# Output projection by block products: third's blocks in two tasks, the norm's weights on POOL, an earlier input load

## The chip, the core and the metric

The kernel runs on one NeuronCore of a Trainium2 chip. The metric is the time of one execution on the device in microseconds (us). The core's engines are TensorE (PE in the profile, its weight loads PEld), VectorE (DVE), ScalarE (ACT), GpSimd (POOL) and SyncE (SP), which here only issues DMAs. Each engine works through its own instructions in program order and waits on semaphores for the others.

## What is computed

One layer of a decoder trunk for one sequence of 512 tokens and a width of 2048 (all f32): a modulated RMSNorm, one wide input projection, latent attention and a spatial gating unit side by side, their gated sum `merged`, an output projection with a gated residual, and a final RMSNorm. The change lies in the last two lines:

```python
merged = jax.nn.sigmoid(g_mla) * y_mla + jax.nn.sigmoid(g_sgu) * y_sgu
x = x + gate[:, None] * (merged @ w_out[l])      # (512, 2048) @ (2048, 2048)
return rmsnorm(x, final_norm_g)                  # y * rsqrt(mean(y*y) + eps) * g
```

## The kernel before

Every f32 matrix product is done as three products of fp32r parts. A tile is split into a high part (a cast on ACT) and a low part (tile minus high part, on DVE); `hilo` (L139) is these two instructions, and `tt` (L122) is DVE's tensor_tensor. The engines' program order is the order in which the Python code issues the instructions; nothing reorders them.

**The output projection.** The 2048 output columns are four column groups of 512 (`columns(cg)`, L1564), the 512 tokens four blocks of 128 (n = 0 to 3), and the 16 chunks of `merged` are `mh[j]`, `ml[j]` (high and low, 128 x 512 tokens each). `left` and `right` are the two halves of 256 tokens. Column groups 0 and 3 are done plainly: `out_granule` (L1470) multiplies two chunks with a weight tile of 128 x 1024 into four PSUM banks, eight granules for each group. Column groups 1 and 2 are done together as a 2 x 2 block product (two halves of the tokens, of the 16 chunks and of the columns) with seven block products in place of eight. They run in the order `seven = (6, 1, 7, 2, 5, 3, 4)` (L1585), each in four granules of one weight tile of 128 x 1024; `steps` (L1587) lists the 28 pairs (product, granule). The sums and differences that this needs are made of three kinds of data:

- Of the chunks: `make_dsum(c)` (L1568) makes three combinations of the chunks c and c + 8 for products 6, 2 and 7 (s1, s2, s4). `make_third(c)` (L1578) makes left half minus right half of chunk c, splits it, and writes it over the right half of `mh[c]`, `ml[c]`. It is a sum on DVE, a difference on DVE, a cast on ACT and the low part on DVE, one behind the other.
- Of the weights: DMAs that add to what is in SBUF, issued by POOL (`chain_load`, `third_add`). `third_load` (L1602) first loads four plain tiles by SP into the space of s4h and s4l, and so waits until product 7 has read them.
- Of the results: `after(p, n2)` (L1691) combines the PSUM banks of the products, on ACT and DVE, into `y_of(col, half, n2)` for the column groups 1 and 2, two halves of the tokens and two blocks in each. They lie in the space of s1h and s1l. `gated` multiplies with the gate row `grow`, and `add_x` (L1683) has POOL issue a DMA that adds the block of x from DRAM.

**The order of work** (L1766). In step s the code first issues the weight split of step s + 2 (`split_step`, a cast on ACT and a low part on DVE, 1024 wide; three buffers, so the cast waits until PE has finished step s - 1), then the weight load three tiles ahead (`take`, on SP), then the 12 matmuls of the granule (six for each of two token blocks; `granule`, L1652), and then the tasks that hang on this step in the dictionary `tasks`. Tasks of a step stand in the order in which they were put in. So the tasks of step s lie between the splits of steps s + 2 and s + 3 on ACT and DVE. Before, the thirds hang on (1,1), (1,3), (7,0), (7,2) and the four granules of product 2; the plain group 3 is finished by `plain_residual(3, n)` at (6,0), (6,2), (1,0) and (7,1), and group 0 between the granules of group 3 (L1634).

**The norm.** A residual is `ps * grow` and then `+ y` (x was loaded into y before). `norm_part` (L1552) squares y on ACT with a sum along the row into `ssy`, and then multiplies y with the norm's weights `gfb` on DVE. For the left token blocks in column groups 1 and 2 the second step is left to the end: `finish_row` (L1720) scales with the row's 1/rms, by ACT ("act"), by DVE's tensor_scalar, or with the weights in one DVE instruction ("last"), and has SP store each piece.

**The end** (L1781). `after(3, .)` forms the right blocks; product 4 then runs for block 2 as a whole and for block 3 in two halves of 256 columns. `left_rows(m)` finishes the two left blocks and `norm_of(2, 1, m)` norms column group 2 of the two right ones, both behind product 4's first four granules; then each right block gets its last residual, norm and stores.

## Time and profile before

| | us |
|---|---|
| median of 3 runs (lowest to highest) | 1613.58 (1613.2 to 1614.93) |
| the profiled execution | 1613.45 |
| its span, first to last instruction | 1611.8 |
| busy time of PE / DVE / ACT / POOL | 1587.3 / 1218.1 / 783.8 / 126.0 |
| first matmul of the block products | 1511.43 |
| end of the last matmul | 1595.68 |

Times in the profile are us from the start of the span. A row of the timeline gives start, duration, engine, line in the kernel, operation, out <- in by the program's names (without buffer numbers), shapes and types, and in brackets how long the engine had been idle and which instruction released it. The line is often that of a helper (L123 is `tt`, L140 the cast in `hilo`), so the names of the tiles tell what it is: w0, w1, w2 are the buffers of split weights, wraw and raw unsplit ones, sig is a temporary, s1 and s4 hold the combined chunks and later the results, gbc is `grow`. PE's durations overlap: matmuls of 512 columns start 0.23 us apart and last 0.39.

### The profile page before, as it was taken

The numbers are of one execution on the slowest core, as the hardware profiler recorded it, in microseconds if no ns is written. First come the engines' busy times: TensorE is split into PE (matmuls) and PEld (weight loads), VectorE is DVE, ScalarE is ACT, GpSimd is POOL, SyncE is SP. The second block draws the span as 40 slices with busy tenths as digits, with TensorE's granted clock in tenths as the row PEclk, the third lists the DMA queues.
The fourth block names the chain that finished last, engine by engine and source line by source line (L and its number), as shares of the span: only waits on it lengthen the run. The fifth ranks groups of instructions, "written<-read, shape, count | busy, mean of one in ns | idle before, by whom it ended". The sixth has DMA issues, their size and how long they took to land.

```text
span 1611.8 us, 27090 instructions
## 1 busy us (share of the span) xinstructions
PE 1587.3 (98%) x10688; PEld 1478.9 (92%) x10688; DVE 1218.1 (76%) x1815; ACT 783.8 (49%) x1311; POOL 126.0 (8%) x152
## 2 busy tenths in 40 slices
PE   9999999999999999999999999999999999999996
PEld 8888889999999999999999999999888898888865
DVE  8989679658777777777777777666878887867776
ACT  4443334455545454454555554554655545534444
POOL 0000000001111111111111101112000000000011
PEclk9999999999999999999999999999999999999998
DMA  9988488568899998898887988888422322338587
GB/s 379 353 298 314 171 281 322 169 201 208 218 249 252 233 247 214 233 255 213 228 248 199 271 244 221 231 196 198 133 92 82 105 89 83 97 137 255 132 216 175
DMA packets 127519, 340.14 MB, mean 211 GB/s; under 512 B 14600, under 2 KB 36384, under 8 KB 121120
## 3 DMA queue, kind: packets, MB, share of 16 engines
q1 hardware_dynamic: 106064, 269.72, 47.9%
q0 software_dynamic: 21328, 68.69, 24.3%
q8 instruction: 84, 1.38, 0.3%
q14 instruction: 43, 0.35, 0.1%
HBM read 314.43 MB, written 23.93 MB: 210 GB/s over the span
## 4 chain that ended last, share of the span: by engine, by line
PE 87%; DVE 4%; DMA 3%; issue 3%; ACT 3%; POOL 1%; SPq 0%; DVEq 0%; ACTq 0%; POOLq 0%
PE ps L1256 14%; PE ps L1258 14%; PE ps L1257 14%; PE ps L136 14%; PE ps L137 13%; PE ps L135 13%; PE ps L1418 1%; DMA lat<-v_d 1%; PE ps L1381 1%; PE ps L1382 1%; DMA wsr<-in_wsT 1%; DMA wraw<-in_w 1%; DVE w1l L123 1%; PE ps L819 0%; DMA s1l<-in_xn 0%
## 5 line engine op out<-in xcount | busy, mean ns | idle before, releaser
L1256 PE MATMUL ps<-hh,w0h 128*128 128x256 f32 x416 | 118.5, 285 | 0.9 <-DVE lat L123 0.9
L1257 PE MATMUL ps<-hl,w0h 128*128 128x256 f32 x416 | 117.7, 283 | 0.0
L1258 PE MATMUL ps<-hh,w0l 128*128 128x256 f32 x416 | 117.7, 283 | 0.0
L1256 PE MATMUL ps<-hh,w2h 128*128 128x256 f32 x400 | 113.5, 284 | 0.0
L1256 PE MATMUL ps<-hh,w1h 128*128 128x256 f32 x400 | 113.4, 283 | 0.0
L1258 PE MATMUL ps<-hh,w2l 128*128 128x256 f32 x400 | 113.2, 283 | 0.0
L1257 PE MATMUL ps<-hl,w1h 128*128 128x256 f32 x400 | 113.2, 283 | 0.0
L1257 PE MATMUL ps<-hl,w2h 128*128 128x256 f32 x400 | 113.2, 283 | 0.0
L1258 PE MATMUL ps<-hh,w1l 128*128 128x256 f32 x400 | 113.2, 283 | 0.0
L126 DVE SCALAR_TENSOR_TENSOR wada<-wada,cact 128x2048 f32<-128x2048 f32 x47 | 107.1, 2281 | 0.0
L123 DVE TENSOR_TENSOR w2l<-raw,w2h 128x1024 fp32r<-128x1024 f32 x60 | 73.4, 1224 | 41.2 <-ACT w2h L638 39.1
L105 ACT CAST w0h<-wraw 128x1024 fp32r<-128x1024 f32 (+3 forms) x69 | 63.6, 922 | 82.3 <-PE ps L137 44.2
L105 ACT CAST w1h<-wraw 128x1024 fp32r<-128x1024 f32 (+3 forms) x69 | 58.6, 849 | 91.8 <-PE ps L137 36.3
L106 DVE TENSOR_TENSOR w0l<-wraw,w0h 128x1024 fp32r<-128x1024 f32 (+3 forms) x69 | 72.7, 1054 | 36.9 <-ACT w0h L105 36.5
L106 DVE TENSOR_TENSOR w1l<-wraw,w1h 128x1024 fp32r<-128x1024 f32 (+3 forms) x69 | 67.0, 971 | 35.7 <-ACT w1h L105 34.7
L618 POOL DMA_DIRECT2D wraw<-in_wh x67 | 59.3, 939 | 439.4 <-DVE w0l L123 212.4
L135 PE MATMUL ps<-w0h,hh 128*128 128x256 f32 (+3 forms) x288 | 92.7, 322 | 0.0
L136 PE MATMUL ps<-w0l,hh 128*128 128x256 f32 (+3 forms) x288 | 92.7, 322 | 0.1
L137 PE MATMUL ps<-w0h,hl 128*128 128x256 f32 (+3 forms) x288 | 92.4, 321 | 0.0
L135 PE MATMUL ps<-hh,w1h 128*128 128x512 f32 x226 | 89.8, 397 | 0.0
L136 PE MATMUL ps<-hl,w1h 128*128 128x512 f32 x226 | 88.3, 391 | 0.8 <-DVE hl L126 0.8
L123 DVE TENSOR_TENSOR w1l<-wraw,w1h 128x1024 fp32r<-128x1024 f32 x48 | 58.8, 1225 | 40.0 <-ACT w1h L638 37.5
(479 smaller groups left out, 5525.1 us busy)
## 6 DMA issues: line engine op xcount, KB each, us to landing
raw<-in_wh SPq DMA_DIRECT2D x105, 512.0 KB, 6.9
wada<-in_wada SPq DMA_DIRECT2D x47, 1024.0 KB, 7.4
wraw<-in_wh POOLq DMA_DIRECT2D x67, 512.0 KB, 7.1
wraw<-in_wh SPq DMA_DIRECT2D x45, 512.0 KB, 8.0
raw<-in_wh POOLq DMA_DIRECT2D x42, 512.0 KB, 8.2
wraw<-in_wo SPq DMA_DIRECT2D x28, 512.0 KB, 4.1
half<-in_w SPq DMA_DIRECT2D x35, 256.0 KB, 5.4
wraw<-in_w SPq DMA_DIRECT2D x16, 512.0 KB, 8.5
```

The source lines that it names most:

```text
L105: self.nc.scalar.copy(hi[:, :n], raw[:, :n])
L106: self.nc.vector.tensor_tensor(out=lo[:, :n], in0=raw[:, :n], in1=hi[:, :n].bitcast(F32), op=ALU.subtract)
L123: DVE.tensor_tensor(out=out, in0=in0, in1=in1, op=op)
L126: DVE.scalar_tensor_tensor(out=out, in0=in0, scalar=scalar, in1=in1, op0=op0, op1=op1, **kw)
L135: PE.matmul(ps, ah, bh, start=start, stop=False)
L136: PE.matmul(ps, ah, bl, start=False, stop=False)
L137: PE.matmul(ps, al, bh, start=False, stop=stop)
L618: q_.dma_start(t, wh[h, n, q // 10 - 1], **eng)
L1256: PE.matmul(ps, wH[:, sl], xh, start=st, stop=False, skip_group_check=True)
L1257: PE.matmul(ps, wH[:, sl], xl, start=False, stop=False, skip_group_check=True)
L1258: PE.matmul(ps, wL[:, sl], xh, start=False, stop=sp, skip_group_check=True)
L1381: PE.matmul(ps, q2[:, q], krh[:, :n], start=False, stop=False)
```

## The change

Three edits, all in the output projection:

1. `make_third` becomes two tasks. `third_diff(c)` makes the difference into a tile of its own (`dif`, 128 x 256); `third_split(c)`, one step later, casts it and makes the low part. Chunk 0 begins at (1,2), chunk 1 at (7,0), and then one at each step up to (2,2).
2. `norm_part` becomes `square` (ACT) and `gain` (the product with `gfb`, on DVE or on the engine given). For the plain groups the gain is a task one step behind the square; group 0's gains move in the same way, and `plain_residual(3, n)` moves to (6,0), (6,2), (6,3) and (1,0), its gains to (6,1), (6,3), (1,0) and (1,1). For column groups 1 and 2 of the left blocks, and for column group 2 of the right ones, the gain is done by POOL (six tiles of 128 x 512). The left blocks' pieces that were "last" become tensor_scalar on DVE.
3. x for column group 1 of the right blocks is loaded by SP when product 1 begins, as a plain load, and added with the gate by `residual` after product 3, in place of `gated` and an adding DMA of POOL. In the end section both `left_rows` come behind product 4's second granule, and both `norm_of(2, 1, m)` behind its fourth.

```diff
--- before.py
+++ after.py
@@ -1549,17 +1549,17 @@
         load_before(go[3, 2 + i], chain_load, i, 11)
         load_before(go[3, min(4 + i, 7)], chain_load, i, 12)
 
-    def norm_part(n, part, cols, y, last):
+    def square(n, part, y):
         junk = nt(tp, [P, S], F32, "sig", bufs=3)[:, :y.shape[-1]]
         ACT.activation(junk, y, AF.Square, accum_out=ssy[:, n, part:part + 1])
-        if not last:
-            tt(y, y, gfb[:, cols], ALU.mult)
-
-    def residual(n, part, cols, y, ps, last=False):
+
+    def residual(cols, y, ps):
         t = nt(tp, [P, S], F32, "sig", bufs=3)[:, :y.shape[-1]]
         tt(t, ps, grow[:, cols], ALU.mult)
         tt(y, t, y, ALU.add)
-        norm_part(n, part, cols, y, last)
+
+    def gain(cols, y, eng=None):
+        (eng or DVE).tensor_tensor(out=y, in0=y, in1=gfb[:, cols], op=ALU.mult)
 
     def columns(cg, o=0, w=S):
         return slice(cg * S + o, cg * S + o + w)
@@ -1575,11 +1575,16 @@
         for n, src in (("s1", b[:, right]), ("s2", a[:, left]), ("s4", b[:, left])):
             hilo(dsum[n + "h"][:, c], dsum[n + "l"][:, c], src)
 
-    def make_third(c):
+    def third_diff(c):
         a = nt(tp, [P, S], F32, "sig", bufs=3)
         tt(a, mh[c].bitcast(F32), ml[c].bitcast(F32), ALU.add)
-        tt(a[:, left], a[:, left], a[:, right], ALU.subtract)
-        hilo(mh[c][:, right], ml[c][:, right], a[:, left])
+        dif[c] = nt(dp[0].p, [P, 256], F32, "dif")
+        tt(dif[c], a[:, left], a[:, right], ALU.subtract)
+
+    def third_split(c):
+        hilo(mh[c][:, right], ml[c][:, right], dif.pop(c))
+
+    dif = {}
 
 
     seven = (6, 1, 7, 2, 5, 3, 4)
@@ -1627,7 +1632,11 @@
         hilo(hi, lo, raw)
 
     def plain_residual(cg, n):
-        residual(n, cg and 1, columns(cg), yt[cg][:, n], plain[cg][n])
+        residual(columns(cg), yt[cg][:, n], plain[cg][n])
+        square(n, cg and 1, yt[cg][:, n])
+
+    def plain_gain(cg, n):
+        gain(columns(cg), yt[cg][:, n])
 
     plain = {0: pso, 3: [bank_at(4 + k) for k in range(NB)]}
     for cg in (0, 3):
@@ -1636,6 +1645,8 @@
             if cg == 0 and i > 3:
                 make_dsum(i - 4)
             elif cg and i % 2 == 0:
+                if i > 0:
+                    plain_gain(0, i // 2 - 1)
                 make_dsum(4 + i // 2)
             elif cg:
                 plain_residual(0, i // 2)
@@ -1673,6 +1684,8 @@
         elif p == 1:
 
             yp[0], yp[1] = (nt(dp[0].p, [P, 2, 2 * S], F32, t) for t in ("s1h", "s1l"))
+            for n2 in range(2):
+                DMA.dma_start(y_of(1, 1, n2), xn[2 + n2][:, columns(1)])
             pair_banks["y"] = [bank_at(k) for k in (2, 3)]
         elif p == 5:
             pair_banks["w"] = [bank_at(k) for k in (4, 5)]
@@ -1702,8 +1715,6 @@
             gated(y, y, 2)
             add_x(0, n2, 2)
         elif p == 3:
-            gated(y_of(1, 1, n2), b, 1)
-            add_x(1, n2, 1)
             y = y_of(2, 1, n2)
             tt(y, y, b, ALU.subtract)
             gated(y, y, 2)
@@ -1715,7 +1726,8 @@
             add_x(0, n2, 1)
 
     def norm_of(col, half, n2):
-        norm_part(2 * half + n2, 2 if half else col + 1, columns(col), y_of(col, half, n2), half == 0)
+        square(2 * half + n2, 2 if half else col + 1, y_of(col, half, n2))
+        gain(columns(col), y_of(col, half, n2), nc.gpsimd)
 
     def finish_row(n, r, pieces):
 
@@ -1734,7 +1746,7 @@
         ACT.activation(r, r, AF.Sqrt, bias=eps, scale=1.0 / D)
         DVE.reciprocal(out=r, in_=r)
         finish_row(n, r, [(columns(cg), yt[cg][:, n] if cg in yt else y_of(cg, 0, n), k)
-                          for cg, k in ((0, "act"), (1, "last"), (2, "last"), (3, "act"))])
+                          for cg, k in ((0, "act"), (3, "act"), (2, "dve"), (1, "dve"))])
 
 
     tasks = {}
@@ -1743,9 +1755,13 @@
         tasks.setdefault((p, i), []).append(lambda: f(*a))
 
     for c in range(8):
-        task((1, 1, 7, 7, 2, 2, 2, 2)[c], (1, 3, 0, 2, 0, 1, 2, 3)[c], make_third, c)
-    for n, (p, i) in enumerate(((6, 0), (6, 2), (1, 0), (7, 1))):
-        task(p, i, plain_residual, 3, n)
+        at_ = (6, 8, 9, 10, 11, 12, 13, 14)[c]
+        task(*steps[at_], third_diff, c)
+        task(*steps[at_ + 1], third_split, c)
+    for n in range(4):
+        task(*steps[(0, 2, 3, 4)[n]], plain_residual, 3, n)
+        task(*steps[(1, 3, 4, 5)[n]], plain_gain, 3, n)
+    task(*steps[0], plain_gain, 0, 3)
     for i in range(4):
         task(6, min(i + 2, 3), chain_load, i, 22)
         task(2, min(i + 2, 3), chain_load, i, 21)
@@ -1780,6 +1796,8 @@
 
     for n2 in range(2):
         after(3, n2)
+    for n2 in range(2):
+        residual(columns(1), y_of(1, 1, n2), pair_banks["y"][n2])
     half = S // 2
     for n2 in range(2):
         n = 2 + n2
@@ -1790,19 +1808,21 @@
             ps = bank_at((6, 7, 0)[n2 + part])[:, :w]
             for i in range(4):
                 granule(4, i, [ps], [n2], slice(o, o + w))
-                if n2 == 0 and i == 3:
+                if (n2, i) == (0, 1):
                     for m in range(2):
                         left_rows(m)
+                if (n2, i) == (0, 3):
+                    for m in range(2):
                         norm_of(2, 1, m)
             yo = y[:, o:o + w]
             last = o + w == S
             if last:
                 DVE.tensor_reduce(out=r, in_=ssy[:, n, 0:3 + part], axis=AX.X, op=ALU.add)
                 ts(r, r, 1.0 / D, EPS, ALU.mult, ALU.add)
-            t = nt(tp, [P, S], F32, "sig", bufs=3)[:, :w]
-            tt(t, ps, grow[:, columns(1, o, w)], ALU.mult)
-            tt(yo, t, yo, ALU.add)
-            norm_part(n, 3 + part, columns(1, o, w), yo, last)
+            residual(columns(1, o, w), yo, ps)
+            square(n, 3 + part, yo)
+            if not last:
+                gain(columns(1, o, w), yo)
         ACT.activation(r, ssy[:, n, 3 + part:4 + part], AF.Sqrt, bias=r, scale=1.0 / D)
         DVE.reciprocal(out=r, in_=r)
         pieces = [(columns(0), yt[0][:, n], "act"), (columns(3), yt[3][:, n], "dve"), (columns(2), y_of(2, 1, n2), "dve")]
```

## The prediction

> **What bounds the kernel now.** I read first the chain of waits that ended last, by engine: it consists of matmuls, so up to the last matmul every idle moment of TensorE is lost time. The edits begin where the output projection's plain groups end; from there I read a table of stretches, one for each block product in the order 6, 1, 7, 2, 5, 3 (then 4) and one for what follows the last matmul. Its columns: stretch, length, busy time of PE, PEld, DVE, ACT and POOL, granted clock, DMA share, GB/s.
>
> ```profile
> PE 87%; DVE 4%; DMA 3%; issue 3%; ACT 3%; POOL 1%; SPq 0%; DVEq 0%; ACTq 0%; POOLq 0%
> ...
> 1511.43:1522.67 11.24, 11.24 (x50) 9.04 (x49) 8.87 (x11) 5.43 (x8) 2.54 (x3) 1.00 0.92 160
> 1522.67:1533.55 10.88, 10.88 (x49) 9.01 (x48) 7.69 (x10) 5.67 (x9) 0.00 (x0) 1.00 0.65 202
> 1533.55:1546.83 13.28, 11.93 (x50) 8.69 (x48) 9.12 (x14) 5.65 (x10) 0.00 (x0) 1.00 0.51 160
> 1546.83:1560.73 13.90, 13.14 (x48) 10.27 (x49) 10.81 (x15) 5.01 (x7) 6.03 (x7) 0.88 1.00 258
> 1560.73:1573.34 12.61, 11.70 (x49) 8.78 (x48) 10.08 (x15) 8.19 (x11) 2.56 (x3) 1.00 1.06 229
> 1573.34:1584.22 10.88, 10.88 (x49) 9.01 (x48) 10.79 (x12) 6.22 (x11) 1.70 (x2) 1.00 0.60 106
> 1595.68:1611.80 16.12, 0.00 (x0) 0.00 (x0) 7.51 (x20) 4.32 (x13) 0.00 (x0) 0.64 0.57 207
> ```
>
> Undisturbed, product 6 takes 11.24 us (four granules of 2.81) and product 1 takes 10.88 (2.72). Products 7 and 2 use the same kind of operands as 6, products 5 and 3 as 1; so 7, 2 and 5 lose 2.04, 2.66 and 1.73, in all **6.4 us**. That is the most that splitting the third's task can win. The timeline of PE shows whom it waited for, and a stretch after it the clock:
>
> ```profile
> 1534.23 0.50 PE L1661 MATMUL ps<-w0l,s4h 128*128 128x512 f32 x1 [0.28 <-DVE w0l L123]
> 1546.83 0.50 PE L1660 MATMUL ps<-w2h,s2h 128*128 128x512 f32 x1 [0.73 <-ACT w2h L140]
> 1548.09 0.50 PE L1661 MATMUL ps<-w2l,s2h 128*128 128x512 f32 x1 [0.76 <-DVE w2l L123]
> ...
> 1549.00:1552.00 3.00, 3.00 (x9) 2.32 (x8) 2.01 (x4) 2.30 (x3) 1.03 (x2) 0.50 0.93 311
> ```
>
> PE is late because the weights' splits are late, and behind two holes of 0.73 and 0.76 us the clock stood at 0.50 for 3 us: 1.5 of the 6.4 us. The splits are late because of how DVE and ACT take turns (their timelines, DVE first):
>
> ```profile
> 1518.38 1.23 DVE L123 TENSOR_TENSOR w1l<-wraw,w1h 128x1024 fp32r<-128x1024 f32 x1 [0.16 <-ACT w1h L140]
> 1519.52 0.68 DVE L123 TENSOR_TENSOR sig<-ps,gbc 128x512 f32<-128x512 f32 x1
> 1520.24 0.69 DVE L123 TENSOR_TENSOR y<-sig,y 128x512 f32<-128x512 f32 x1
> 1521.72 0.69 DVE L123 TENSOR_TENSOR y<-y,gfb 128x512 f32<-128x512 f32 x1 [0.79 <-ACT sig L1554]
> 1522.65 1.22 DVE L123 TENSOR_TENSOR w0l<-wraw,w0h 128x1024 fp32r<-128x1024 f32 x1 [0.24 <-ACT w0h L140]
> 1524.00 1.23 DVE L123 TENSOR_TENSOR w2l<-wraw,w2h 128x1024 fp32r<-128x1024 f32 x1
> 1528.76 1.22 DVE L123 TENSOR_TENSOR w1l<-wraw,w1h 128x1024 fp32r<-128x1024 f32 x1 [0.73 <-ACT w1h L140]
> 1530.62 0.42 DVE L123 TENSOR_TENSOR sig<-sig 128x256 f32<-128x256 f32 x1
> 1531.52 0.43 DVE L123 TENSOR_TENSOR g<-sig,b 128x256 fp32r<-128x256 f32 x1 [0.47 <-ACT b L140]
> 1532.95 1.23 DVE L123 TENSOR_TENSOR w0l<-wraw,w0h 128x1024 fp32r<-128x1024 f32 x1 [1.01 <-ACT w0h L140]
> ...
> 1520.96 0.63 ACT L1554 ACTIVATE sig<-y 128x512 f32<-128x512 f32 x1 [2.62 <-DVE y L123]
> 1521.59 1.03 ACT L140 CAST w0h<-wraw 128x1024 fp32r<-128x1024 f32 x1
> 1527.21 0.57 ACT L1695 COPY s1l<-ps 128x512 f32<-128x512 f32 x1
> 1527.68 1.05 ACT L140 CAST w1h<-wraw 128x1024 fp32r<-128x1024 f32 x1
> ```
>
> With a third in the granule, DVE makes the difference, waits 0.47 for ACT's cast, subtracts, then waits 1.01 for the next split's cast: 4.19 us from 1528.76 to 1532.95 where PE needs 2.72.
>
> **The thirds.** With the difference a granule ahead, a granule costs DVE 1.14 (1518.38 to 1519.52) for the split, 0.34 for the third's low part (0.43 less the same overlap of 0.09) and 0.72 + 0.34 for the next difference: 2.5 us, less than 2.72, and neither cast waits for DVE. I take the three products' waits as gone. What covers this is DVE's spare time.
>
> **The plain residuals.** Residual, Square on ACT, then the next split's cast on ACT: the cast stands behind the Square, and the Square behind the residual. From 1518.38 to 1522.65 that is 4.27 us, and the weighting with gfb at 1521.72 lies in the hole, free. The change takes it out of the hole and puts it, 0.60 us each, a granule later in front of the next residual; and the residuals move to granules 0, 2, 3 and 4. So the low parts of the splits start: (6,1) at 1512.0 (three tasks earlier, 0.6 of weighting is added; 1511.40 before); (6,2) 1.14 later; (6,3) 1517.4 (+4.28, one weighting still fits the hole); (1,0) 1519.2 (+1.14 + 0.60); (1,1) 1523.4 (+4.27); (1,2) 1528.3 (+4.27 + 0.60); (1,3) 1533.7 (+0.47 more, the copy of 1527.21). Before, the last two were 1524.00 and 1528.76. Each is ready 1.22 later. PE wants them with its second matmul, at 1528.3 and, 1.4 us late by then, at 1532.5: it waits 1.3 and 2.5 us, with 0.1 for each restart **4.0 us**. The new holes (about 0.9, 1.3 and 0.9) are larger than those that cost the clock before, so I add 1.5: **5.5 us lost in place of 6.4**.
>
> The Trainium skill, TensorE: Matmul & The Clock Gate, section HAM oscillation, gives as the rule that only idle gaps above some 3.4 us lower the clock; the 0.50 behind gaps of 0.73 and 0.76 us disagrees, and by the rule the 1.5 us would go (second rival).
>
> **The loads behind it.** Product 3's weights come by DMA, and there the gain is capped (a stretch; the two queues between 1545 and 1580 us with packets, MB and share of the 16 engines' time; then SP's, POOL's and ACT's rows):
>
> ```profile
> 1547.00:1577.50 30.50, 28.82 (x115) 22.33 (x116) 24.88 (x32) 15.53 (x20) 8.59 (x10) 0.94 1.04 239
> ...
> q0 software_dynamic: 1440, 4.72, 69.1%
> q1 hardware_dynamic: 835, 3.03, 24.9%
> ...
> 1545.89 0.81 SPq L1606 DMA_DIRECT2D s4h<-in_wo  x2
> 1548.33 0.85 POOL L1539 DMA_DIRECT2D raw<-in_wo  x1 [28.98 <-DVE w2l L123]
> 1577.99 1.05 ACT L140 CAST w0h<-s4l 128x1024 fp32r<-128x1024 f32 x1 [1.82 <-DMA s4l<-in_wo]
> ```
>
> The DMA engines are full for 30 us. The last weights of product 3 land at 1577.95, and cast, subtraction and matmuls follow closely; a faster PE would wait here. The loads at 1545.89 reuse s4h, so they start when product 7 ends: 4.0 + 1.5 - 1.1 (what 7 lost before its last matmul) = 4.4 us later. One accumulating load (the one of 1548.33, which waits only for the split of (2,0)) now runs before them. The accumulating queue, q0, took 69.1% of 35 us, 24 us, for 4.72 MB: 2.7 us for a block of 512 KB. So the last landing comes 4.4 - 2.7 = 1.7 us later. Today DVE is 1.0 us late for that block behind older splits, which it no longer is, and PE needs it only 0.5 us after it is ready; with these 1.5 us off, product 3 ends **0.2 us later**, though TensorE alone would be 0.9 earlier. The bounds: 0.9 earlier, if the loads keep up; 1.7 later, if none of that slack comes back.
>
> **The tail.** Before, the last x add decides (POOL's issues, the chain's DMA step, the Squares that follow):
>
> ```profile
> 1582.89 0.84 POOL L1686 DMA_DIRECT2D s1h<-in_xn  x1 [2.74 <-DVE s1h L123]
> 1587.97 7.06 DMA s1l<-in_xn
> 1595.11 0.63 ACT L1554 ACTIVATE sig<-s1l 128x512 f32<-128x512 f32 x1 [0.20 <-DMA s1l<-in_xn]
> 1598.22 0.63 ACT L1554 ACTIVATE sig<-s1l 128x512 f32<-128x512 f32 x1 [2.40 <-DVE s1l L123]
> ```
>
> Two of four adds go: x is loaded by SP at product 1's start, as soon as product 6 has read s1l (1522.7), ahead of a weight load that waits for the split of (1,2) anyway, so that queue loses nothing. But POOL now runs four products before it issues the two adds left. No such product is in the trace: DVE's 0.69 bounds it below; above, a select of a quarter of the width (0.49, next fence) times four, 1.97. I take 1.3, between the two. Counted from product 3's end (1584.22): POOL is free at -0.5, three products end at 3.4, the fourth waits for its tile's landing and Square and ends at 4.95; adds at 4.95 and 5.5, landing after 5.5 us (between 4.1 and 7.06) at 11.0; the row's own Square then stands at 12.0 (ACT's four scalings and two Squares end there too) against 14.0 now: 2.0 us won. If POOL waits for DVE's four two-operand instructions of 0.69 in that stretch, the landing is 2.8 us later: 0.5 lost. Rows for the wait (POOL, then DVE):
>
> ```profile
> 1.23 0.49 POOL masks.py:199 TENSOR_SCALAR_AFFINE_SELECT ident<-ident 128x128 f32<-128x128 f32 x1
> 10.09 1.23 POOL L356 TENSOR_SCALAR_AFFINE_SELECT mask<-mask 128x128 f32<-128x128 f32 x1 [7.45 <-PE ps L342]
> ...
> 9.94 1.23 DVE L106 TENSOR_TENSOR w0l<-wraw,w0h 128x1024 fp32r<-128x1024 f32 x1 [0.41 <-ACT w0h L105]
> ```
>
> The same select took 1.23 instead of 0.49 and ended 0.15 after DVE's instruction. I take the middle, **0.8 won**. By the Trainium skill, SBUF — State Buffer, section SBUF: two separate sides, the two engines share a port pair as an exclusive lock; the select's row agrees, and by it the tail would lose 0.5 instead.
>
> What else moves in the tail I cost at nothing: the two products with grow go from in front of the last x adds to behind them and gain two additions (four instructions, 2.7 us of DVE, while the adds land); the left rows' pieces become plain scalings, their weights having gone to POOL; their order only sorts the stores on SP. The cover is the landing; without it the additions cost 1.4 us.
>
> **Sum.** +0.2 - 0.8 = -0.6 us on the profiled execution (span 1611.8, time 1613.45); the median of the runs lies 0.13 above that: 1613.0. Its own range, from the bounds: 1610.7 to 1615.8.
>
> **Rivals.** *No stall in product 1* (20%): for it, DVE is busy only 7.69 of 10.88 us there; against it, the order on ACT. Then PE regains 6.4, the loads start 1.1 earlier with 2.7 us of traffic less in their way, and with the slack of 1.5 product 3 ends 5.3 earlier, with the tail 6.1: 1607.5. *No half clock* (18%): the loads start 1.5 earlier than in the forecast, so product 3 ends 1.3 earlier than now: 1611.5; with POOL unhindered 1610.3. For it: the clock held through the hole of 0.28 us; against it: 0.73 and 0.76 were enough. *POOL holds up the adds* (20%, slower): its four products stand in front of add_x on one queue. Above some 1.9 us each the last landing passes today's; at 2.5 and with half of DVE's waits the fourth ends near 11, the row's Square comes 4 us later: 1617.8. For it the 1.23 us select, against it DVE's 0.69.
>
> **How the numbers follow.** The forecast has 42%. A difference below 0.2% (3.2 us) can't be told from none. Faster: the first rival and a fifth of the second, 24%; slower: the third, 20%; same: 56%. The range, 1609 to 1617.5, reaches halfway into the outer two.
>
> **What would show it.** Right: PE holes in granules 2 and 3 of product 1, with the split's low part at 1528 and 1533; none in 7 and 2; third's loads issued near 1550; POOL's adds behind its products. Wrong: product 1 at 10.9 us; product 3 ending before 1581; Square of the row before product 3's end + 11.

## The result and the profile after

| | before | after |
|---|---|---|
| median (lowest to highest), 14 runs each, us | 1613.82 (1612.99 to 1616.12) | 1615.76 (1614.81 to 1617.07) |
| the profiled execution, us | 1613.45 | 1615.73 |
| its span, us | 1611.8 | 1613.9 |

The ratio of the times is 1.0012, with a 95% interval from 1.0003 to 1.002. So the change made the kernel slower by some 2 us (0.12%); the forecast had 0.6 us faster.

The table of stretches after the change (columns as in the prediction): products 6, 1, 7 and 2, then 5 and 3 together, then from product 4's start to the end:

```profile
1511.73:1522.97 11.24, 11.24 (x49) 9.04 (x48) 8.51 (x10) 5.03 (x9) 2.58 (x3) 1.00 0.91 157
1522.97:1539.46 16.49, 13.57 (x50) 9.99 (x49) 11.66 (x15) 7.35 (x12) 0.00 (x0) 0.90 0.63 185
1539.46:1550.70 11.24, 11.24 (x50) 9.04 (x49) 8.86 (x15) 6.18 (x9) 0.86 (x1) 1.00 0.67 186
1550.70:1561.94 11.24, 11.24 (x50) 9.04 (x48) 10.34 (x17) 5.42 (x8) 5.29 (x6) 1.00 1.03 282
1561.94:1585.67 23.73, 22.41 (x98) 17.86 (x97) 17.19 (x20) 12.68 (x18) 4.53 (x6) 1.00 0.89 182
1585.67:1613.90 28.23, 11.45 (x73) 10.17 (x71) 17.72 (x35) 10.80 (x26) 9.63 (x8) 0.75 0.61 177
```

Products 7 and 2 now run undisturbed (11.24 each; 4.70 us won), and product 1 loses 5.61 us. Products 5 and 3 take 23.73 instead of 23.49, and what follows takes 28.23 instead of 27.58. With the later start of product 6 (0.30 us, 1511.43 to 1511.73; it varies by more than that between the runs below, 1511.23 to 1512.01 with the same code ahead of it) that is 0.30 + 5.61 - 4.70 + 0.24 + 0.65 = 2.1 us, the whole difference of the spans. PE's timeline shows whom it waited for:

```profile
1529.93 0.50 PE L1672 MATMUL ps<-w2l,b 128*128 128x512 f32 x1 [0.77 <-DVE w2l L123]
...
1534.03 0.50 PE L1671 MATMUL ps<-w1h,b 128*128 128x512 f32 x1 [1.31 <-ACT w1h L140]
1535.29 0.80 PE L1672 MATMUL ps<-w1l,b 128*128 128x512 f32 x1 [0.76 <-DVE w1l L123]
...
1571.29 0.50 PE L1672 MATMUL ps<-w1l,b 128*128 128x512 f32 x1 [0.76 <-DVE w1l L123]
...
1583.03 0.50 PE L1672 MATMUL ps<-w0l,b 128*128 128x512 f32 x1 [0.57 <-DVE w0l L123]
```

The first three holes lie in granules 2 and 3 of product 1, the fourth in product 5, the last in product 3. The low parts of the two splits behind the first three, in DVE's timeline:

```profile
1528.65 1.23 DVE L123 TENSOR_TENSOR w2l<-wraw,w2h 128x1024 fp32r<-128x1024 f32 x1 [1.73 <-ACT w2h L140]
...
1534.01 1.23 DVE L123 TENSOR_TENSOR w1l<-wraw,w1h 128x1024 fp32r<-128x1024 f32 x1 [2.21 <-ACT w1h L140]
```

The last two holes are late loads. From the timelines: SP's issues of the first two of product 3's plain blocks and of product 5's last block, POOL's last adding load, and ACT's casts of the two late blocks (first product 5's, then product 3's); then, from the view of DMA issues, the last two adding loads of product 3 with KB each and the median us from issue to landing; then the step for the first of them in the chain of waits:

```profile
1550.66 0.85 SPq L1611 DMA_DIRECT2D s4h<-in_wo  x2
1558.90 0.33 SPq L1603 DMA_DIRECT2D wraw<-in_wo  x1
1566.65 1.21 POOL L1614 DMA_DIRECT2D s4l<-in_wo  x1
1568.93 1.05 ACT L140 CAST w1h<-wraw 128x1024 fp32r<-128x1024 f32 x1 [5.22 <-DMA wraw<-in_wo]
1580.67 1.05 ACT L140 CAST w0h<-s4l 128x1024 fp32r<-128x1024 f32 x1 [1.72 <-DVE s1h L123]
```

```profile
s4l<-in_wo POOLq DMA_DIRECT2D x2, 512.0 KB, 16.4
```

```profile
1558.06 18.80 DMA s4l<-in_wo
```

Product 5's last block took 10 us from its issue at 1558.90 to the cast at 1568.93. The cast at 1580.67 names a DVE instruction that it does not read; with a median of 16.4 for two loads of which one took 18.80, the other took 14.0 and landed at 1566.65 + 14.0 = 1580.65, so it was the load that the cast waited for.

The end in the timelines, DVE first, then POOL, then ACT (the second left row's scalings, the first right Square, and the Square of the row's last residual):

```profile
1585.36 0.68 DVE L123 TENSOR_TENSOR s1l<-s1l,ps 128x512 f32<-128x512 f32 x1
1586.08 3.75 DVE L123 TENSOR_TENSOR s1l<-s1l,gbc 128x512 f32<-128x512 f32 x1
1589.76 0.67 DVE L123 TENSOR_TENSOR s1l<-s1l,ps 128x512 f32<-128x512 f32 x1
1590.46 1.08 DVE L123 TENSOR_TENSOR s1l<-s1l,gbc 128x512 f32<-128x512 f32 x1
...
1594.11 0.15 DVE L1745 TENSOR_REDUCE ry<-ssy 128x1 f32<-128x4 f32 x1
...
1585.17 4.11 POOL L1562 TENSOR_TENSOR s1h<-s1h,gfb 128x512 f32<-128x512 f32 x3
1589.59 1.41 POOL L1562 TENSOR_TENSOR s1h<-s1h,gfb 128x512 f32<-128x512 f32 x1 [0.31 <-ACT sig L1554]
1590.93 1.78 POOL L1699 DMA_DIRECT2D s1l<-in_xn  x2
...
1596.58 1.34 ACT L1738 ACTIVATE y<-y,ry 128x512 f32<-128x512 f32 x2 [0.23 <-DVE ry L1747]
1597.82 0.61 ACT L1554 ACTIVATE sig<-s1l 128x512 f32<-128x512 f32 x1
...
1600.52 0.63 ACT L1554 ACTIVATE sig<-s1l 128x512 f32<-128x512 f32 x1 [1.13 <-DVE s1l L123]
```

A product of POOL takes some 1.4 us (4.11 for three of them). While three of them ran back to back, DVE's product of two SBUF operands, 0.69 us elsewhere, took 3.75, and the next one 1.08: 3.45 us more. The instructions with one operand in PSUM (ps) beside them kept their 0.68. Behind the held ones stand the four residual instructions, and behind these the left rows' first reduction: 8.44 us after product 4's start, where before it came 3.37 after it. The first right Square (1597.82) follows ACT's scalings of the left rows without a wait. The x add that it needs was issued at 1590.93 and landed 4.3 us later (from the view of DMA issues), near 1595.2. The chain of waits that ended last, which before passed through an x add's landing, now runs through DVE and the left rows instead.

### The profile page after: what moved, and what is told of

Same layout as the page of the kernel before. It is cut to its first block, busy times and chain, and to the rows that moved or that the text cites. A ratio compares the mean times of both kernels' runs of the same rounds, so it can differ in the third digit from the quotient of the medians.

```text
span 1613.9 us, 27096 instructions
## 1 busy us (share of the span) xinstructions
PE 1587.4 (98%) x10688; PEld 1479.0 (92%) x10688; DVE 1219.1 (76%) x1815; ACT 782.8 (49%) x1311; POOL 133.0 (8%) x156
## 4 chain that ended last, share of the span: by engine, by line
PE 88%; DVE 5%; DMA 3%; ACT 2%; issue 1%; POOL 0%; SPq 0%; DVEq 0%; ACTq 0%; POOLq 0%
PE ps L1256 15%; PE ps L1258 15%; PE ps L1257 15%; PE ps L136 12%; PE ps L137 12%; PE ps L135 12%; DMA s4l<-in_wo 1%; PE ps L1418 1%; DVE wada L126 1%; PE ps L1381 1%; PE ps L1382 1%; DVE t L123 1%; DMA wraw<-in_w 1%; DVE s1l L123 1%; PE ps L819 1%
```

## The experiments

Each experiment was timed beside the kernel before, whose median was then 1613.9 to 1614.5; the ratios are to that. The lengths are those of one profiled execution of each kernel. They come from the first matmul of each product in PE's timeline (product 6 takes 11.24 in all of them); "to the end" is product 4's start to the end of the span. Undisturbed, product 1 takes 10.88, 7 and 2 together 22.48, 5 and 3 together 21.76.

| kernel | product 1 | 7 and 2 | 5 and 3 | to the end | median | ratio to before (95%) |
|---|---|---|---|---|---|---|
| before | 10.88 | 27.18 | 23.49 | 27.58 | | |
| after | 16.49 | 22.48 | 23.73 | 28.23 | 1615.76 | 1.0012 (1.0003 to 1.002) |
| e1, weights on DVE | 16.48 | 22.48 | 23.68 | 30.43 | 1617.74 | 1.0019 (1.001 to 1.0028) |
| e2, plain part back | 10.89 | 22.73 | 25.31 | 28.18 | 1612.36 | 0.9985 (0.9976 to 0.9993) |
| e3, tail back | 16.51 | 22.50 | 23.50 | 28.22 | 1615.35 | 1.0007 (0.9998 to 1.0016) |
| e4, thirds only | 10.88 | 22.68 | 25.83 | 28.06 | 1611.41 | 0.9981 (0.9973 to 0.999) |
| e5, thirds and early load | 10.89 | 23.12 | 24.96 | 26.83 | 1610.65 | 0.9976 (0.9967 to 0.9986) |
| e6, e5 with left rows first | 10.88 | 22.67 | 25.82 | 28.12 | 1611.74 | 0.9984 (0.9975 to 0.9993) |
| e7, e4 without the thirds' adds | 10.88 | 23.04 | 25.57 | 26.68 | 1609.79 | 0.9971 (0.996 to 0.9983) |
| e8, e4 with one block early | 10.89 | 26.08 | 22.81 | 27.41 | 1612.59 | 0.9988 (0.998 to 0.9997) |
| e9, e5 with another load order | 10.88 | 22.73 | 26.85 | 26.84 | 1612.17 | 0.9984 (0.9975 to 0.9992) |
| e10, after with that order | 14.97 | 22.48 | 26.69 | 28.21 | 1617.34 | 1.0016 (1.0008 to 1.0025) |
| e11, after, weights in the hole | 12.97 | 22.49 | 25.31 | 28.25 | 1613.47 | 0.9993 (0.9984 to 1.0001) |
| e12, e5 with merged weights | 10.89 | 22.87 | 25.05 | 24.84 | 1608.45 | 0.9964 (0.995 to 0.9977) |

**e1: weights on DVE.** Is DVE's wait for POOL what the tail loses?

```diff
     def norm_of(col, half, n2):
         square(2 * half + n2, 2 if half else col + 1, y_of(col, half, n2))
-        gain(columns(col), y_of(col, half, n2), nc.gpsimd)
+        gain(columns(col), y_of(col, half, n2))
```

> The changed kernel with the four products with the norm's weights (left tiles and the two right ones) on DVE instead of POOL; all else as changed. Theory (POOL's back-to-back products hold DVE's two-operand instruction: 3.75 us where it takes 0.69): the long instruction is gone, no two-operand instruction of 128x512 in product 4 is above 0.9 us; DVE does four products more, 2.8 us, of which about 1 was idle anyway, so the stretch from product 4's start to the end is 27.0 to 27.8 us instead of 28.2: 1614.6 to 1615.4. Rival A (the x adds queued behind POOL's products set the end): the adds are issued some 3 us earlier and the end follows them, 1612.5 to 1613.5. Rival B (POOL is irrelevant, DVE's own amount of work sets the tail): 2 us more on DVE, 1617 to 1618.

The long instruction is gone, as the theory wants; the same product beside an idle POOL:

```profile
1590.40 0.69 DVE L123 TENSOR_TENSOR s1l<-s1l,gbc 128x512 f32<-128x512 f32 x1
```

But the time grew by 2 us, to what rival B had said: the fourth left product waits for the last left Square on DVE's own queue, and the two right ones stand in the chain of the end. With the weights as products of their own, POOL is the better place, in spite of the wait. The theory left out that in the kernel before, in "last", the weights of the left pieces had cost little extra: 0.75 us for a scaling with weights, where a plain one takes 0.48.

**e2, e3, e4: the parts undone.** e2 puts the plain residuals and weightings back, e3 the whole tail, e4 both, which leaves the thirds alone.

```diff
+++ e2
-                if i > 0:
-                    plain_gain(0, i // 2 - 1)
...
                 plain_residual(0, i // 2)
+                plain_gain(0, i // 2)
...
-        task(*steps[(0, 2, 3, 4)[n]], plain_residual, 3, n)
-        task(*steps[(1, 3, 4, 5)[n]], plain_gain, 3, n)
-    task(*steps[0], plain_gain, 0, 3)
+        at_ = steps[(0, 2, 4, 9)[n]]
+        task(*at_, plain_residual, 3, n)
+        task(*at_, plain_gain, 3, n)
...
+++ e3
-        gain(columns(col), y_of(col, half, n2), nc.gpsimd)
+        if half:
+            gain(columns(col), y_of(col, half, n2))
...
-                          for cg, k in ((0, "act"), (3, "act"), (2, "dve"), (1, "dve"))])
+                          for cg, k in ((0, "act"), (1, "last"), (2, "last"), (3, "act"))])
...
-            for n2 in range(2):
-                DMA.dma_start(y_of(1, 1, n2), xn[2 + n2][:, columns(1)])
...
+            gated(y_of(1, 1, n2), b, 1)
+            add_x(1, n2, 1)
...
-    for n2 in range(2):
-        residual(columns(1), y_of(1, 1, n2), pair_banks["y"][n2])
...
-                if (n2, i) == (0, 1):
+                if (n2, i) == (0, 3):
                     for m in range(2):
                         left_rows(m)
-                if (n2, i) == (0, 3):
-                    for m in range(2):
                         norm_of(2, 1, m)
```

> The changed kernel with the plain groups' residuals and weightings back in their old slots, each weighting right behind its own Square; thirds in two tasks, weights on POOL and the early load stay. Theory (the moved residuals and weightings alone make the 5.6 us lost in product 1, half clock included): product 1 takes 10.9 to 11.5 us at clock 1.00, products 7 and 2 stay at 11.24, third_load is issued near 1545; the accumulating loads give back a part, and product 3 ends 3.5 to 5 us earlier: 1610.8 to 1612.3. Rival A (product 3's weights come by a DMA stream that was full anyway, so that the loads cap the end): product 3 ends at most 1.5 us earlier, 1614.3 or more. Rival B (thirds at the new slots load DVE in product 1, not the weightings): product 1 still takes 14 us or more, 1615 to 1616.

> The changed kernel with the tail as before: weights in the left rows' last scaling and on DVE for the right tiles, no early load of x, left rows behind product 4's granule 3; thirds in two tasks and the moved plain residuals stay. Theory (the tail of the change loses 0.65 us from product 4's start, by DVE waiting for POOL): product 4's start to the end 27.5 to 27.7 us, product 1 still 16.4, product 4 starts near 1585.5: 1615.0 to 1615.3. Rival (the early load's place in SP's queue delays the take for product 5 and with it the 2 us lost in products 5 and 3): product 4 starts 0.5 to 1 earlier as well, 1614.2 to 1614.7. If the tail's edits do win something, as the forecast had it, 1616.4 to 1616.8.

> The kernel before with one part of the change alone: each third's block in two tasks a granule apart, at the new slots. Theory: products 6, 1, 7, 2 take 11.2, 10.9, 11.2, 11.2 us, the half clock in product 2 goes; product 3 ends 4 to 5 us before that of the kernel before less 1 us for its loads, and the tail is the old one of 27.6: 1609.5 to 1611.0. If the parts add up, it is the time of the changed kernel plus the differences that the two runs with one part undone show. Rival (the loads cap): 1612.5 to 1613.8, as before.

e2's stretches: product 1, products 5 and 3, product 4's start to the end:

```profile
1523.69:1534.58 10.89, 10.89 (x49) 9.01 (x48) 8.96 (x11) 6.10 (x9) 0.00 (x0) 1.00 0.81 261
1557.31:1582.62 25.31, 22.65 (x98) 17.86 (x96) 18.88 (x22) 12.86 (x18) 4.52 (x6) 1.00 0.93 187
1582.62:1610.80 28.18, 11.46 (x73) 10.17 (x71) 17.72 (x35) 10.82 (x26) 9.64 (x8) 0.77 0.60 177
```

The whole stall of product 1 is the plain part's doing, half clock included: 16.49 falls to 10.89, with the thirds in their new slots. Of the 5.6 us won, products 5 and 3 give 1.6 back (25.31 instead of 23.73), with the DMA engines 0.93 busy: the loads follow product 7's end only in part. That is the theory, at the low end of what it had product 4 win (3.77 us, measured from product 6's start; 3.5 to 5 expected); 1612.36 instead of at most 1612.3.

e3 refutes my theory of the tail: with the old tail product 4's start to the end is still 28.22, not 27.6. The change's tail as a whole neither won nor lost; the 0.65 us against the kernel before are there with the old tail too, and 0.48 of them with the thirds alone (e4: 28.06 with the old code). In e4 the x add that the first right Square waits for took 6.1 us from its issue, before the change 5.4; why it takes longer wasn't settled. The early load's place in SP's queue, e3's rival, is worth some 0.2 us (23.73 against 23.50).

e4 is faster than the kernel before by 0.19%: the thirds alone were the good part, though 0.4 us above the range of the theory: product 4 starts 2.16 us earlier, counted from product 6's start, and not 3 to 4, because products 5 and 3 give back more (25.83), and the end takes 0.48 more.

**e5, e6: the early load.** e4's plain slots and "last", with x loaded early; in e6 both left rows come ahead of the two moved residuals, and the two right norms behind these.

```diff
+++ e5, against e4
+            for n2 in range(2):
+                DMA.dma_start(y_of(1, 1, n2), xn[2 + n2][:, columns(1)])
...
-            gated(y_of(1, 1, n2), b, 1)
-            add_x(1, n2, 1)
...
+    for n2 in range(2):
+        residual(columns(1), y_of(1, 1, n2), pair_banks["y"][n2])
+++ e6, against e5
-    for n2 in range(2):
-        residual(columns(1), y_of(1, 1, n2), pair_banks["y"][n2])
...
                     for m in range(2):
                         left_rows(m)
+                    for m in range(2):
+                        residual(columns(1), y_of(1, 1, m), pair_banks["y"][m])
+                    for m in range(2):
                         norm_of(2, 1, m)
```

> The thirds in two tasks and the early load of x (its two tiles by SP, their residual behind the last x adds), without the moved plain residuals and without weights on POOL. Compared with the thirds alone (1611.41; 28.06 us from product 4's start to the end). Theory: the early load takes two of four x adds away, but the four instructions that it moves behind the others stand in front of the left rows' first reduction on DVE, which now comes 2.7 us later after product 4's start; DVE is the bound, so the stretch is 27.4 to 28.4 us, 1610.8 to 1611.8. Rival (the x adds' landing sets the end, as the forecast had it): 2 us won, 1609.4.

> As the run with the early load alone, but both left rows are finished first and the moved residuals come after them, before the right rows' Squares. Theory (DVE's order sets the tail): the first reduction is back at 3 to 3.5 us after product 4's start and the residuals lie in the time of the x adds' landing; product 4's start to the end 26.8 to 27.6 us: 1610.2 to 1611.0. Rival (the landing): the same as the run with the early load alone, within 0.3 us.

```profile
1582.77:1609.60 26.83, 11.46 (x73) 10.17 (x71) 16.45 (x37) 11.03 (x26) 1.70 (x2) 0.79 0.64 186
```

This is the stretch of e5 from product 4's start. The early load alone wins 28.06 - 26.83 = 1.23 us, more than the theory allowed (27.4 at best) and less than the rival. Put against e2, which has the same load and POOL's weights with the left rows' new place, 28.18 - 26.83 = 1.35 us is what those cost. e6 refutes the reason that I gave for e5: it is slower (28.12), where the theory had it faster. ACT and DVE of e5, then the same two of e6:

```profile
1586.02 0.63 ACT L1554 ACTIVATE sig<-s1h 128x512 f32<-128x512 f32 x1 [2.89 <-DMA s1h<-in_xn]
...
1586.76 1.28 ACT L1746 ACT_TABLE_LOAD   x1
...
1587.78 0.15 DVE L1745 TENSOR_REDUCE ry<-ssy 128x1 f32<-128x4 f32 x1
```

```profile
1585.67 0.63 ACT L1554 ACTIVATE sig<-s1h 128x512 f32<-128x512 f32 x1 [2.94 <-DMA s1h<-in_xn]
...
1588.04 0.16 DVE L1747 RECIPROCAL ry<-ry 128x1 f32<-128x1 f32 x1 [3.10 <-ACT ry L1746]
```

The left rows can't begin before ACT has the last left x add and its table: in e5 the table is there at 1588.04, and DVE's reduction, behind the four residual instructions, ends at 1587.93. The residuals fill a gap that DVE has anyway. In e6 DVE idles 3.10 us there and does the residuals later, on the path. So the first reduction may come 5.0 us after product 4's start for nothing; at 8.44, where DVE's wait for POOL puts it, it is 3.4 us late.

**e7, e8: the loads.** e7 leaves out the thirds' adds, so that its output lacks these terms and only its time counts; e8 loads one of the four blocks in product 1, into the free half of s1l (`third0()` is that half, `halves` a view of a block).

```diff
+++ e7, against e4
-        task((2, 5)[i // 2], (2, 3, 0, 1)[i], third_add, i)
...
+++ e8, against e4
...
-        for i in range(4):
+        for i in range(1, 4):
             DMA.dma_start(third[i // 2][:, i % 2], w_block(12, i))
...
+            DMA.dma_start(third0(), halves(w_block(12, 0)))
             pair_banks["y"] = [bank_at(k) for k in (2, 3)]
...
-        task((2, 5)[i // 2], (2, 3, 0, 1)[i], third_add, i)
+        task((1, 2, 5, 5)[i], (1, 3, 0, 1)[i], third_add, i)
```

> The thirds in two tasks alone, and without the four accumulating loads that add the second blocks to product 3's weights (these terms of the output are left out). Theory (the full DMA engines cap products 5 and 3, which lose 4.1 us with the thirds alone and 2.0 in the changed kernel): without 2 MB of the traffic products 5 and 3 take 21.8 to 22.5 us together, no wait of PE in them, and product 4 starts 3.4 to 4.1 us earlier than with the thirds alone: 1607.2 to 1608.3. Rival (the splits on ACT and DVE cap them, not the loads): 25 us or more, 1610.7 to 1611.7.

> The thirds in two tasks alone, with the first of product 3's four blocks loaded and added to in product 1, into the half of s1l that is free there until product 3 has ended; the same bytes in all, 1 MB of them in an earlier stretch. Theory (the DMA engines are full from product 7's end until product 3's last weights have landed): 1 MB at 210 to 240 GB/s is 4.4 to 5 us; products 5 and 3 lose 1 us or less instead of 4.1, and product 4 starts 3 to 4 us earlier: 1607.4 to 1608.6. Rival (what is late is the last block in the order of POOL's queue, not the bytes): products 5 and 3 lose 3 us or more, 1610.5 to 1611.5.

The theory of e7 missed: products 5 and 3 take 25.57 us, not 21.8 to 22.5. Product 3 runs undisturbed (10.90 us), but product 5 still loses 3.8 us, some of it at half clock: its last block, issued at 1555.35, is there no sooner than 9 us later.

```profile
1564.44 1.04 ACT L140 CAST w1h<-wraw 128x1024 fp32r<-128x1024 f32 x1 [5.85 <-DMA wraw<-in_wo]
```

So the adds cap product 3, and the plain load of the block (5,3), behind everything that is under way by then, caps product 5. The stretch to the end shrank by 1.4 us too: without the adds the last left Square starts 1.3 us after product 4's start, and in e4 3.1.

e8, products 7 and 2, then 5 and 3; behind them ACT's cast of the last block of product 7:

```profile
1534.50:1560.58 26.08, 24.53 (x97) 19.15 (x96) 20.96 (x34) 12.43 (x19) 5.18 (x6) 0.93 0.87 228
1560.58:1583.39 22.81, 22.10 (x97) 17.95 (x96) 17.50 (x20) 12.64 (x18) 4.26 (x5) 1.00 0.71 140
```

```profile
1539.43 1.05 ACT L140 CAST w0h<-wraw 128x1024 fp32r<-128x1024 f32 x1 [2.36 <-DMA wraw<-in_wo]
```

1 MB less in the full stretch takes the loss of products 5 and 3 from 4.1 to 1.05 us, as expected. The time did not follow: the same MB now delays the weight loads of product 7. The cast shown starts 2.15 us later than in e4 (1537.28), so does the first cast for product 2 (1545.59 against 1543.45), and product 2 starts behind two holes, again at half clock.

**e9, e10: another order of the same bytes**, on e5 and on the changed kernel.

```diff
     def third_load(part):
         if part == 0:
             third.extend(nt(dp[0].p, [P, 2, GW], F32, t) for t in ("s4h", "s4l"))
-        for i in range(4):
+        for i in range(2 * part, 2 * part + 2):
...
-    task(2, 0, third_load)
+    task(2, 0, third_load, 0)
+    task(2, 2, third_load, 1)
...
-        task((2, 5)[i // 2], (2, 3, 0, 1)[i], third_add, i)
+        task((2, 5)[i // 2], (2, 3, 0, 0)[i], third_add, i)
```

> Thirds in two tasks and the early load (1610.65), with two loads in another order, the bytes the same: the last two blocks of product 3's first loads go behind the load of product 5's last block on SP, and the last accumulating load of product 3 goes to POOL one granule earlier, ahead of an x add that waits for DVE. Theory (what is late in products 5 and 3 is these two transfers, which queue behind others that are wanted later): products 5 and 3 together take 21.8 to 23 us instead of 24.96, product 4 starts 2 to 3 us earlier, the rest stays at 26.4 to 27 us: 1607.6 to 1608.7. Rival (the engines are full and only the sum of the bytes counts): product 4 starts within 0.5 us of before, 1610.2 to 1611.2.

> The changed kernel, whole, with the same other order of loads. Theory: its 1.97 us lost in products 5 and 3 fall to 0.8 or less; product 1 (16.5 us) and the stretch from product 4's start (28.2) stay: 1614.0 to 1614.9. Rival (only the sum of the bytes counts): 1615.4 to 1616.2.

Both lost. In e9, SP's issue of (5,3), its cast, and POOL's wait for product 3's third block:

```profile
1555.91 0.33 SPq L1603 DMA_DIRECT2D wraw<-in_wo  x1
1565.11 1.04 ACT L140 CAST w1h<-wraw 128x1024 fp32r<-128x1024 f32 x1 [5.96 <-DMA wraw<-in_wo]
1569.35 0.86 POOL L1614 DMA_DIRECT2D s4l<-in_wo  x1 [14.86 <-DMA s4l<-in_wo]
```

The block (5,3) still took 9 us with 1 MB less of plain loads ahead of it: what is left ahead of it are POOL's adding loads. The two blocks put behind it came later, and product 3 with them. Both times lie above even the rivals' ranges (1612.17 against at most 1611.2, 1617.34 against at most 1616.2). The rival is nearer: it is the bytes under way that count, and a load moved back is late by itself.

**e11: weightings back in the hole, residuals in the new slots.**

```diff
-                if i > 0:
-                    plain_gain(0, i // 2 - 1)
...
                 plain_residual(0, i // 2)
+                plain_gain(0, i // 2)
...
-        task(*steps[(1, 3, 4, 5)[n]], plain_gain, 3, n)
-    task(*steps[0], plain_gain, 0, 3)
+        task(*steps[(0, 2, 3, 4)[n]], plain_gain, 3, n)
```

> The changed kernel with each weighting right behind its own Square again, in the residuals' new slots. It tells the weightings from the residuals' slots. By the forecast's own sum (0.6 us for each weighting that has left the hole, 1.2 by granules 2 and 3 of product 1) the low parts of the splits of (1,2) and (1,3) start near 1527.4 and 1532.6 instead of 1528.65 and 1534.01; product 1 loses 1.3 to 2.8 us instead of 5.6: 1612.6 to 1614.0. Rival (the residuals' slots alone make the stall): product 1 still loses 4.5 us or more, 1615.0 to 1616.0. Rival (the weightings alone): product 1 takes 11.5 us or less, 1611.8 to 1612.8, the time with both put back.

```profile
1527.38 1.23 DVE L123 TENSOR_TENSOR w2l<-wraw,w2h 128x1024 fp32r<-128x1024 f32 x1 [0.25 <-ACT w2h L140]
...
1532.14 1.23 DVE L123 TENSOR_TENSOR w1l<-wraw,w1h 128x1024 fp32r<-128x1024 f32 x1 [0.72 <-ACT w1h L140]
```

With the start of product 6 taken off (1511.84), the low parts start 1.4 and 2.0 us sooner than in the changed kernel, and product 1 loses 2.09 us, at full clock. Of the 4.1 us that the changed kernel's stall takes without the half clock (14.97 - 10.88, from e10), the weightings out of the hole make about 2.0 and the residuals' slots 2.1. Both parts of the forecast's reason count.

**e12: the weights merged.** The right rows' column group 2 gets its weights in the last scaling.

```diff
-        if half:
-            gain(columns(col), y_of(col, half, n2))
...
-        pieces = [(columns(0), yt[0][:, n], "act"), (columns(3), yt[3][:, n], "dve"), (columns(2), y_of(2, 1, n2), "dve")]
+        pieces = [(columns(0), yt[0][:, n], "act"), (columns(3), yt[3][:, n], "dve"), (columns(2), y_of(2, 1, n2), "last")]
```

> Thirds in two tasks and the early load (1610.65 us, 26.83 from product 4's start to the end), and the weights of the right rows' third column group are merged into their last scaling, as those of the left rows already are: two products of 0.69 us leave the chain of the end, two scalings grow from 0.48 to 0.75. Theory (DVE's in-order chain sets the tail): 1.38 less, 0.54 more, the stretch from product 4's start takes 25.8 to 26.3 us: 1609.6 to 1610.2. Rival (the stores or ACT set the end): within 0.2 us of 1610.65.

```profile
1580.26:1605.10 24.84, 11.46 (x73) 10.17 (x71) 15.60 (x35) 10.72 (x26) 1.70 (x2) 0.78 0.67 201
```

The stretch from product 4's start fell by 1.99 us, more than the 0.84 of the sum: in e5 each of the two products had also made DVE wait 0.57 us for its Square, with the next reduction behind it. The median is 1608.45 us, a ratio of 0.9964 (0.995 to 0.9977), below the theory's 1609.6 to 1610.2; the profiled execution was the fastest of five, 1606.78. The version that beats both kernels has the thirds in two tasks, the early load, no moved residuals, and no product for the weights that can be merged.

## Why the prediction came out as it did

**The thirds** were right: products 7 and 2 lost 4.70 us together and lose nothing now.

**The plain residuals** were right: 5.5 us lost in product 1 was forecast, 5.61 came, with the low parts at 1528.65 and 1534.01 (forecast 1528.3 and 1533.7, and the stage began 0.30 later). e11 and e2 show that it was the reasons given. The 1.5 of the half clock was right in part by luck: it came in the profiles of the changed kernel, e1 and e3, and not in that of e10, which has the same holes.

**The loads** were mis-sized, in the term "product 3 ends 0.2 us later": it was 1.15 (73.94 us instead of 72.79 from product 6's start to product 4's), inside the bounds of -0.9 to 1.7. The last landing came 2.4 us later in the stage instead of 1.7 (1580.65 against 1577.95, less 0.30), and 1.25 of the slack came back instead of 1.5. The forecast also counted product 5's 1.73 us among the thirds' waits and took them as gone; 1.10 was still lost there (11.98 us), now to the late load of its own last block, a transfer that the forecast did not follow. That the loads cap the gain was right; e4 and e2 show it, and e7 that two different transfers do it.

**The tail** is the step that failed. "0.8 won" became 0.65 lost from product 4's start. POOL's price (1.3; some 1.4 measured) and the adds' issue (4.95 after product 3's end; 1590.93 is 5.26 after it) were right, but I let only POOL wait for DVE, and it was DVE that waited, 3.45 us by its rows. The path was wrong with it: I had the end hang on the last landing, with ACT's scalings done at the same time, and it hung on DVE's chain through the left rows, which made these scalings late; the row's own Square came 14.85 us after product 3's end instead of 12.0. "What else moves in the tail I cost at nothing" fell as well: the four residual instructions have a cover (e5), but not behind a held DVE. In its place the runs put this: the early load wins 1.23, POOL's weights with the left rows' new place cost 1.35, so that the tail's edits are worth nothing (28.23 against e3's 28.22), and some 0.5 is lost with the thirds alone (e4), for which the forecast had no term. No run left the products on POOL and took only the overlap away, so the 3.45 is read from the rows; e1 shows only that the instruction is back at 0.69 when POOL is idle. The forecast's 0.5 lost for a hindered POOL doesn't follow from its terms either: 2.0 won and a landing 2.8 later give 0.8 lost. The middle would then have been 0.6 won instead of 0.8, which changes neither the direction nor the cause.

**The rivals.** The slower one, POOL holding up the adds, named the right engine with the wrong road: its products were well below 1.9 us each. "No stall in product 1" did not come (16.49 us). "No half clock" was true of e10 and not of the profiled changed kernel, see below.

## What to carry to other kernels

An instruction that moves out of another engine's waiting time costs its full length, even if the engine is busy for only 71% of the stretch (7.69 of 10.88 us here): look for what stands in the hole before calling an engine's spare time free. When work goes to POOL, ask which of DVE's instructions read two SBUF operands in that stretch, and what is queued behind the first of them; merging a factor into a scaling that is done anyway is cheaper than either engine. Where DMA engines are full, a stall removed upstream comes back in part at the next load, and reordering or advancing loads only moved it here (e8 to e10): count the bytes under way when the wanted one is issued.

## What the runs showed of the hardware

**DVE held by POOL.** DVE's product of two SBUF operands waited through three back-to-back POOL products (3.75 us instead of 0.69, and 3.75 or 3.76 in e2, e10 and e11, which have the same tail); it ended 0.55 us after the third. DVE instructions with one operand in PSUM kept 0.67 to 0.68 beside them. The Trainium skill, SBUF — State Buffer, section SBUF: two separate sides, says that a DVE instruction with two SBUF inputs and a GpSimd one exclude each other for a whole instruction. The rows agree. Whether DVE gets in between two POOL products is not settled by them: there it did not, but later in the same trace it did (POOL's last two products, then DVE):

```profile
1598.61 2.94 POOL L1562 TENSOR_TENSOR s1l<-s1l,gfb 128x512 f32<-128x512 f32 x2 [5.90 <-ACT sig L1554]
...
1599.54 0.89 DVE L123 TENSOR_TENSOR s1l<-sig,s1l 128x512 f32<-128x512 f32 x1
```

POOL's first product ended at 1599.88, DVE's at 1600.43, again 0.55 later, and POOL's second took 1.71 us instead of some 1.4. What decides it no run here shows.

**The half clock is not a matter of the holes' size.** The changed kernel in granule 3 of product 1, then e10 in the same place and over the whole of product 1:

```profile
1535.50:1538.50 3.00, 3.00 (x8) 2.33 (x9) 2.96 (x5) 1.25 (x2) 0.00 (x0) 0.50 0.71 183
```

```profile
1535.80:1538.22 2.42, 2.42 (x12) 1.94 (x12) 2.39 (x4) 0.83 (x1) 0.00 (x0) 1.00 0.68 184
1523.25:1538.22 14.97, 12.04 (x50) 8.85 (x49) 10.14 (x13) 6.94 (x11) 0.00 (x0) 1.00 0.60 184
```

Up to there the two kernels are the same, and their holes too (0.77, 1.31, 0.76 and 0.76, 1.33, 0.76 us). One execution went to 0.50 and took 16.49 us, the other did not and took 14.97: 1.52 us, the price that the forecast had set. Over other runs, too, the size does not tell: e2's pair of holes in product 5, 1.23 and 0.76 us, left the clock at 1.00, and e4's, 0.75 and 0.76, was followed by 0.50 for some 3 us. What decides it no run here shows. The Trainium skill, TensorE: Matmul & The Clock Gate, section What's actually happening, describes an activity window that runs free of the kernel, of some 3.4 us; a decision by the window's phase would fit two such executions, and half-clock stretches of about 3 us, but this is not shown.
